# RWKV's outputs: split where they are made instead of stored and loaded again

## The chip, the core and the metric

One core of a Trainium2 chip runs the whole program. The metric is the device time of one execution in microseconds (us). The median of three runs of the kernel before is 2764.43 us (2764.06 to 2771.8).

## What is computed

Two layers over 256 latent and 256 context tokens, width 1024. Each layer has a half-step SwiGLU FFN, three parallel token mixers on one input projection (attention, RG-LRU, RWKV-7), and a second FFN half-step. The change is at the end of the third mixer, where its output is normed per head, gated, and merged with the two others:

```python
def _rwkv_mixer(zr, zrc, mu, w_up, w0, a_up, a0, g_up, k_k, k_a, r_k, ln_g, ln_b, need_ctx):
    ...
    for d in range(2):                                   # both directions
        o_c_d, s_c = _rwkv_scan(s0, rc, w_c, k_c, vc, kkc, a_c, rev)
        o_l_d, _ = _rwkv_scan(s_c, r, w_l, k_l, v, kk, a_l, rev)
        term = o_l_d + _rwkv_bonus(r, k_l, v, r_k)
        o = term if o is None else o + term
    y = (_head_groupnorm(o, ln_g, ln_b) * gate).astype(zr.dtype)

def _gated_merge(outs, zg, proj, w_o):
    g = jax.nn.sigmoid(zg.reshape(zg.shape[0], zg.shape[1], N_BRANCH, D_MODEL))
    acc = g[..., 0, :] * (outs[0] @ proj[0])
    for b in range(1, N_BRANCH):
        acc = acc + g[..., b, :] * (outs[b] @ proj[b])
    return acc @ w_o
```

Context tokens are needed in the first layer only, so the merge runs over 512 columns there and over 256 in the second.

## The kernel before

Activations lie transposed: channels on the 128 partitions, tokens along the free dimension. A mixer's output has 512 channels, in four quarters `f`. All products are made in three passes of a split number: a value is cast to fp32r (`hi`, on ACT) and the rest kept (`lo`, on DVE). `split` (L231) does this for activations, `wload` (L192) for weights, which it loads on SP's queue into three rotating raw tiles `wr`; `wh` and `wl` have two buffers each. `gemm_steps` (L219) issues the three matmuls for each of the k quarters, all on L223.

`rwkv` (L954) is a set of generators that `Weave` lays out on PE by hand, with products of `queue` filled in between: first `tiles` (the gates of the merge, sent to memory as `gd`), then `branch` for the branches 0 (attention) and 1 (RG-LRU). That order is fixed on PE; the other engines' instructions are put in order by the scheduler. `finish` (L1390) ends the mixer: quarters 0 to 2 when their recurrences are done, quarter 3 after the last recurrence `recur(3)`. For each quarter it norms `oc`, multiplies by the gate (L1404) and stores it to `yd` in memory on SP's queue (L1405).

`branch` (L1448) multiplies one branch's output with its projection and adds it, gated, into `acc`. It takes a pair of tiles `yh`, `yl` of four quarters from a pool with two such pairs, and for each quarter loads `yr` from `yd` on ACT's queue (L1456) and splits it:

```python
yh = mp.tile([P, 4, n], F32R, tag="yh", name=f"yh{l}{b}", bufs=2)
yl = mp.tile([P, 4, n], F32R, tag="yl", name=f"yl{l}{b}", bufs=2)
for f in range(4):
    yr = mp.tile([P, n], F32, tag="yr", name=f"yr{l}{b}{f}", bufs=T // n)
    nc.scalar.dma_start(out=yr, in_=yd[b][:, f, qc:])
    split(yh[:, f], yl[:, f], yr)
```

`T // n` is 1 in the first layer and 2 in the second. Then come 8 column tiles `m` of 12 matmuls `bp`; the gates return as `gr` on ACT's queue, and DVE makes `acc` (L1480, branch 0) or `gr` times product (L1482), which POOL adds (L1483). Branch 2, the third, is queued after `rwkv` has ended. `project` (L1485) then loads the stream `x` back from `xd` on ACT's queue (L1495) into memory on the chip that the mixer's tiles held, splits `acc` into `ah`, `al`, and multiplies with `w_out`.

Of the kernel before, what the change touches and what calls it, by code (L numbers as in the profile page):

```python
# [9 lines left out]
F32R = mybir.dt.float32r  # L10
# [5 lines left out]
P = 128  # L16
D = 1024
KD = D // P
T = 512
# [77 lines left out]
def build(tc, a, out, upto=99, dbg=None):  # L97
    nc = tc.nc
    es = ExitStack()
    g = Ctx()  # L100
    with es:
# [13 lines left out]
        def axt(name):  # L115
            return ax.tile([P, T], F32, tag="ax", name=name)
# [102 lines left out]
        def gemm_steps(ps, w, xh, xl, kt, c0=0, c1=T):  # L219
            hi, lo = w  # L220
            for k in range(kt):
                for j, (wt, xt) in enumerate(((hi, xh), (hi, xl), (lo, xh))):
                    nc.tensor.matmul(ps[:, c0:c1], wt[:, k], xt(k)[:, c0:c1],  # L223
                                     start=(k == 0 and j == 0), stop=(k == kt - 1 and j == 2))
                    yield
# [5 lines left out]
        def split(hi, lo, src, eng=None):  # L231
            nc.scalar.copy(hi, src)
            nc.vector.tensor_tensor(lo, src, hi.bitcast(F32), ALU.subtract)
# [16 lines left out]
        for l in range(L):  # L250
            t = vec.tile([P, 2, 72], F32, tag="mT", name=f"mT{l}")
# [311 lines left out]
        def head_bcast(rsE, slot, c0, name):  # L563
            pb = axt(f"hb{name}{slot}")
            nc.tensor.matmul(pb[:, c0:], selT[:, slot], rsE[:].rearrange("p q c -> p (q c)")[:, c0:], start=True, stop=True)
            return pb
# [161 lines left out]
        def step(pe=0.0, area=0.0, dve=0.0, act=0.0, pool=0.0, lag=1, need=()):  # L728


            return pe, area, (dve, act, pool), lag, need
# [219 lines left out]
            v = seg3(ap)  # L951
            return v if d == 0 else v[:, :, ::-1]

        def rwkv(l, rk, z, zd, yd, weave, beside, before_last):  # L954

            full = l < L - 1
            qc = 0 if full else SEG
# [4 lines left out]
            with ExitStack() as ey:  # L962
# [426 lines left out]
                def finish(fs, pool):  # L1389

                    yield step(dve=6.5, act=0.4)
                    rsO = head_rsqrt(pool, pool, "hvo", Y["oss"], qc // P, 1.0 / 64, 64e-5, ALU.add, f"o{l}{fs[0]}")
                    gup = pool.tile([P, T], F32, tag="gup", name=f"gup{l}{fs[0]}")
                    nc.sync.dma_start(out=gup, in_=a["rwkv_g_up"][l])
                    for f in fs:
                        yield step(0.23, 0.5, dve=0.7, act=0.65)
                        pb = head_bcast(rsO, f, qc, f"o{l}")
                        oc = r_[f]
                        nc.vector.tensor_tensor(oc[:, qc:], oc[:, qc:], pb[:, qc:], ALU.mult)
                        nc.scalar.activation(oc[:, qc:], oc[:, qc:], AF.Identity, bias=col(R_LNB + f), scale=col(R_LNG + f))  # L1400
                        yield step(0.85, 2.0, dve=0.7)
                        pg = axt(f"pg{l}{f}")
                        nc.tensor.matmul(pg[:, qc:], gup[:, f * P:(f + 1) * P], sgd[:, qc:], start=True, stop=True)
                        nc.vector.tensor_tensor(oc[:, qc:], oc[:, qc:], pg[:, qc:], ALU.mult)  # L1404
                        nc.sync.dma_start(out=yd[:, f, qc:], in_=oc[:, qc:])  # L1405

                parts = [(-20.0, beside[0](weave.set)), (-18.0, beside[1](weave.set)), (-12.0, setup()), (0.0, outputs())]
                for f in range(4):
# [36 lines left out]
                    done[key], tile_of[key] = 0.0, ps  # L1445
                w = wn_

        def branch(l, b, mp, acc, yd, gd):  # L1448

            qc = 0 if l < L - 1 else SEG  # L1450
            n = T - qc
            yh = mp.tile([P, 4, n], F32R, tag="yh", name=f"yh{l}{b}", bufs=2)
            yl = mp.tile([P, 4, n], F32R, tag="yl", name=f"yl{l}{b}", bufs=2)
            for f in range(4):
                yr = mp.tile([P, n], F32, tag="yr", name=f"yr{l}{b}{f}", bufs=T // n)
                nc.scalar.dma_start(out=yr, in_=yd[b][:, f, qc:])  # L1456
                split(yh[:, f], yl[:, f], yr)
            step = BP_STEP[l]

            def load(m):  # L1460
                return wload(a["branch_proj"][l, b][:, m * P:(m + step) * P], 4)

            def load_gate(m):
                gt = mp.tile([P, n], F32, tag="gt", name=f"gr{l}{b}{m}", bufs=BP_GT[l])
                nc.scalar.dma_start(out=gt, in_=gd[b][:, m, qc:])
                return gt
            ahead = min(BP_GT[l] - 1, KD)
            nxt, gts = load(0), [load_gate(m) for m in range(ahead)]
            for m in range(KD):
                if m + ahead < KD:  # L1470
                    gts.append(load_gate(m + ahead))
                if m % step == 0:
                    ws = nxt
                    nxt = load(m + step) if m + step < KD else None
                w = [t[:, :, m % step * P:(m % step + 1) * P] for t in ws]
                ps = (alt if b == 2 else mmt)(f"bp{l}{b}{m}")
                yield from gemm_steps(ps, w, lambda k: yh[:, k], lambda k: yl[:, k], 4, 0, n)
                gt = gts[m]
                if b == 0:
                    nc.vector.scalar_tensor_tensor(acc[:, m, qc:], gt, 1.0, ps[:, 0:n], ALU.add, ALU.mult)  # L1480
                else:
                    nc.vector.scalar_tensor_tensor(gt, gt, 1.0, ps[:, 0:n], ALU.add, ALU.mult)  # L1482
                    nc.gpsimd.tensor_tensor(acc[:, m, qc:], acc[:, m, qc:], gt, ALU.add)  # L1483
# [72 lines left out]
        for l in range(L):  # L1556
            qc = 0 if l < L - 1 else SEG
            ffn(l, 0, 0, more, (l, 1))
            yd = [dpool.tile([P, 4, T], F32, tag=f"yd{b}", name=f"yd{l}{b}") for b in range(3)]
            gd = [dpool.tile([P, KD, T], F32, tag=f"gd{b}", name=f"gd{l}{b}") for b in range(3)]  # L1560
            zd = dpool.tile([P, 4, T], F32, tag="zd", name=f"zd{l}")
            xd = dpool.tile([P, KD, T], F32, tag="xd", name=f"xd{l}")
            nc.scalar.dma_start(out=xd[:, :, qc:], in_=x[:, :, qc:])
            xp.__exit__(None, None, None)
            with tc.tile_pool(name=f"rk{l}", bufs=1, reuse_waits="tile") as rk:
                z = [None] * 15
                attention(l, yd[0], lambda ap: rwkv_inputs(l, rk, ap, z, zd))
                held["cm"].__exit__(None, None, None)
                done = {}
                queue = [tiles(l, gd, done)]  # L1570

                def fill(n):

                    k = 0
                    while k < n and queue:
                        if next(queue[0], queue) is queue:
                            queue.pop(0)
                        else:
                            k += 1
                    return k  # L1580
                em = ExitStack()
                acc = []

                def before_last():
                    mp = em.enter_context(tc.tile_pool(name=f"mb{l}", bufs=1, side="right", reuse_waits="tile"))
                    acc.append(mp.tile([P, KD, T], F32, tag="acc", name=f"acc{l}"))
                    queue.extend(branch(l, b, mp, acc[0], yd, gd) for b in range(2))
                    acc.append(mp)
                    return mp
                phase[0] = f"r{l}"  # L1590
                with tc.manual_schedule(engines={mybir.EngineType.PE}):
                    weave = Weave(fill, done, (0.226, 0.512) if qc == 0 else (0.118, 0.256))
                    rwkv(l, rk, z, zd, yd[2], weave, lru(l, yd[1], done), before_last)
                    fill(10 ** 6)
                phase[0] = f"m{l}"
            if dbg is not None and upto == l:
                for b in range(3):
                    nc.sync.dma_start(out=dbg["y"][b][:, :, qc:], in_=yd[b][:, :, qc:])
            xp = tc.tile_pool(name=f"xp{l + 1}", bufs=1, reuse_waits="tile")
            x = xp.__enter__().tile([P, KD, T], F32, name=f"x{l + 1}")  # L1600
            queue.append(branch(l, 2, acc[1], acc[0], yd, gd))
            fill(10 ** 6)
            phase[0] = ""
            project(l, acc[0], lambda: (em.close(), hold(l + 1)), xd)
            if dbg is not None and upto == l:
                break
            more = sum([ada(l, 8)] + [ada(l + 1, i) for i in range(3)], []) if l + 1 < L else []
            ffn(l, 1, qc, more, (l + 1, 0) if l + 1 < L else None)
            more = sum([ada(l + 1, i) for i in range(3, 9)], []) if l + 1 < L else []
# [40 lines left out]
```

## Time and profile before

| | before |
|---|---|
| median of three runs | 2764.43 us |
| profiled execution, its own time | 2771.72 us |
| its span | 2769.9 us |
| busy PE, DVE, ACT, POOL | 95%, 63%, 40%, 7% of the span |
| granted TensorE clock, mean | 0.945 of full speed |
| chain that ended last, by engine | PE 19%, DVE 4%, ACT 2%, DMA 1% of the span |
| memory traffic | 318.56 MB read, 20.19 MB written |

Matmuls are pipelined, so PE's busy time is not PE at its peak; a gap is read from the idle time before a matmul, and the clock from the granted share (1.00 is 2.4 GHz, 0.50 is 1.2 GHz). `ACTq` and `SPq` rows are DMA issues. The three branches lie between about 1010 and 1125 us in the first layer, and 2448 and 2535 in the second.

### The profile page before, as it was taken

What the parts mean: (1) busy time and instruction counts of PE and PEld (TensorE: products, weight loads), DVE (VectorE), ACT (ScalarE), POOL (GpSimd) and SP (SyncE); (2) the same over time, 40 slices, a digit from 0 to 9 for tenths busy, and PEclk for the clock granted to TensorE, in tenths of its full rate; (3) what the DMA queues carried; (4) which work ended last, traced back from release to release, by engine and by line L of the source; (5) the groups of instructions that cost most, each with busy time, mean ns of one, the idle gap of its engine ahead of it and who ended that gap; (6) DMA issues with size and microseconds to landing.
All of it is one profiled execution on the core that took longest, in us unless ns stands there. A gap on an engine that the chain in (4) does not pass through costs nothing. (4 is left out here: it accounts for less than half of the span.)

```text
span 2769.9 us, 47656 instructions
## 1 busy us (share of the span) xinstructions
PE 2621.5 (95%) x19761; PEld 2178.9 (79%) x19761; DVE 1732.8 (63%) x2984; ACT 1107.9 (40%) x1817; POOL 191.3 (7%) x197
## 2 busy tenths in 40 slices
PE   7999999999999999999999999999898799887999
PEld 5788888766677777888888978888776588777899
DVE  4867556658756655756654774555757766646565
ACT  4323234337644542332323432323346555433343
POOL 1000002220000001200000100001230000002000
PEclk8999999999889999999999999999999798868999
DMA  7655433123211126825533464544224222126465
GB/s 251 226 159 173 146 104 113 54 69 104 76 44 51 57 84 198 253 62 160 152 108 107 155 184 153 178 148 120 75 77 120 60 76 64 44 80 187 123 183 160
DMA packets 480091, 341.84 MB, mean 123 GB/s; under 512 B 17307, under 2 KB 448884, under 8 KB 479618
## 3 DMA queue, kind: packets, MB, share of 16 engines
q1 hardware_dynamic: 460690, 314.22, 37.6%
q10 hardware_dynamic: 19120, 24.52, 3.1%
q8 instruction: 155, 2.54, 0.4%
q14 instruction: 62, 0.51, 0.1%
q0 software_dynamic: 64, 0.05, 0.0%
HBM read 318.56 MB, written 20.19 MB: 122 GB/s over the span
## 5 line engine op out<-in xcount | busy, mean ns | idle before, releaser
L207 ACT CAST wh<-wr 128x1024 fp32r<-128x1024 f32 (+2 forms) x434 | 436.6, 1008 | 1011.5 <-PE gu L223 353.0
L216 DVE TENSOR_TENSOR wl<-wr,wh 128x1024 fp32r<-128x1024 f32 (+2 forms) x404 | 474.1, 1175 | 291.2 <-ACT wh L207 287.1
L223 PE MATMUL gu<-h_hi,wh 128*128 128x512 f32 (+1 forms) x1528 | 536.9, 353 | 5.7 <-ACT h_hi L389 2.6
L223 PE MATMUL gu<-h_hi,wl 128*128 128x512 f32 (+1 forms) x1528 | 535.6, 351 | 1.7 <-DVE wl L216 1.7
L223 PE MATMUL gu<-h_lo,wh 128*128 128x512 f32 (+1 forms) x1528 | 535.9, 351 | 0.4 <-DVE h_lo L390 0.3
L223 PE MATMUL win<-h_hi,wl 128*128 128x512 f32 (+1 forms) x896 | 331.8, 371 | 3.0 <-DVE wl L216 3.0
L223 PE MATMUL win<-h_hi,wh 128*128 128x512 f32 (+1 forms) x896 | 332.5, 371 | 2.1 <-ACT wh L207 1.7
L223 PEld LDWEIGHTS gu<-h_hi,wh 128*128 128x128 f32 x1528 | 292.1, 192 | 48.7 <-ACT wh L207 6.0
L223 PE MATMUL win<-h_lo,wh 128*128 128x512 f32 (+1 forms) x896 | 329.4, 368 | 0.0
L223 PEld LDWEIGHTS gu<-h_hi,wl 128*128 128x128 f32 x1528 | 293.1, 192 | 39.9 <-DVE wl L216 3.1
L223 PEld LDWEIGHTS gu<-h_lo,wh 128*128 128x128 f32 x1528 | 292.9, 192 | 36.9 <-DVE h_lo L390 0.9
L281 DVE SCALAR_TENSOR_TENSOR adacc<-adw,sc,adacc 128x1024 f32<-128x1024 f32 x196 | 244.7, 1283 | 5.9 <-ACT adacc L279 2.7
L223 PEld LDWEIGHTS win<-h_hi,wl 128*128 128x128 f32 x896 | 176.8, 197 | 44.7 <-issue 21.2
L223 PEld LDWEIGHTS win<-h_hi,wh 128*128 128x128 f32 x896 | 177.1, 198 | 38.0 <-issue 15.8
L223 PEld LDWEIGHTS win<-h_lo,wh 128*128 128x128 f32 x896 | 176.7, 197 | 36.2 <-issue 16.5
L223 PE MATMUL dn<-gh,wh 128*128 128x512 f32 (+1 forms) x560 | 201.0, 359 | 0.0
L223 PE MATMUL dn<-gl,wh 128*128 128x512 f32 (+1 forms) x560 | 199.5, 356 | 0.1
L223 PE MATMUL dn<-gh,wl 128*128 128x512 f32 (+1 forms) x560 | 199.1, 356 | 0.0
L472 DVE SCALAR_TENSOR_TENSOR x<-dn,cf,x 128x256 f32<-128x256 f32 x120 | 53.6, 479 | 113.1 <-PE dn L223 112.8
L506 DVE TENSOR_TENSOR th<-th,gu 128x512 f32<-128x512 f32 (+1 forms) x88 | 54.3, 618 | 111.0 <-PE gu L223 110.6
L223 PEld LDWEIGHTS dn<-gh,wh 128*128 128x128 f32 x560 | 105.2, 188 | 16.9 <-ACT wh L207 1.3
L223 PEld LDWEIGHTS dn<-gh,wl 128*128 128x128 f32 x560 | 105.0, 188 | 16.5
(557 smaller groups left out, 4154.0 us busy)
## 6 DMA issues: line engine op xcount, KB each, us to landing
wr<-ffn_w_gu SPq DMA_DIRECT2D x176, 512.0 KB
adw<-ada_w SPq DMA_DIRECT2D x144, 512.0 KB
wr<-w_in SPq DMA_DIRECT2D x106, 512.0 KB
wr<-ffn_w_d SPq DMA_DIRECT2D x64, 512.0 KB
wr<-ffn_w_d SPq DMA_DIRECT2D x35, 384.0 KB
wr<-w_out SPq DMA_DIRECT2D x17, 512.0 KB
gd<-gt SPq DMA_DIRECT2D x24, 256.0 KB
wr<-branch_proj SPq DMA_DIRECT2D x24, 256.0 KB
```

The source lines that it names most:

```text
L207: nc.scalar.copy(hi[:, 0:w], raw[:, 0:w])
L216: eng.tensor_tensor(lo[:, 0:m], raw[:, 0:m], hi[:, 0:m].bitcast(F32), ALU.subtract)
L223: nc.tensor.matmul(ps[:, c0:c1], wt[:, k], xt(k)[:, c0:c1], start=(k == 0 and j == 0), stop=(k == kt - 1 and j == 2))
L281: nc.vector.scalar_tensor_tensor(acc, w, f, acc, ALU.mult, ALU.add)
L472: nc.vector.scalar_tensor_tensor(x[:, k, cs], ps[:, cs], coef[:, s, k:k + 1], x[:, k, cs], ALU.mult, ALU.add)
L506: nc.vector.tensor_tensor(th[:, c0:], th[:, c0:], pp[1][:, c0:], ALU.mult)
```

## The change

`finish` no longer stores a quarter: it casts and subtracts it at once into the pair `last_y`, which is taken from the pool when the first quarter is ready. `branch` for the third branch gets this pair and loads nothing. The pool keeps two pairs, and `yr` its buffers.

```diff
-        def rwkv(l, rk, z, zd, yd, weave, beside, before_last):
+        def rwkv(l, rk, z, zd, last_y, weave, beside, before_last):
...
                         nc.vector.tensor_tensor(oc[:, qc:], oc[:, qc:], pg[:, qc:], ALU.mult)
-                        nc.sync.dma_start(out=yd[:, f, qc:], in_=oc[:, qc:])
+                        if not last_y:
+                            last_y.extend(pool.tile([P, 4, T - qc], F32R, tag=t, name=f"{t}{l}2", bufs=2) for t in ("yh", "yl"))
+                        split(*[t[:, f] for t in last_y], oc[:, qc:])
...
-        def branch(l, b, mp, acc, yd, gd):
+        def branch(l, b, mp, acc, yd, gd, y=None):
...
-            yh = mp.tile([P, 4, n], F32R, tag="yh", name=f"yh{l}{b}", bufs=2)
-            yl = mp.tile([P, 4, n], F32R, tag="yl", name=f"yl{l}{b}", bufs=2)
-            for f in range(4):
+            yh, yl = y or [mp.tile([P, 4, n], F32R, tag=t, name=f"{t}{l}{b}", bufs=2) for t in ("yh", "yl")]
+            for f in range(0 if y else 4):
...
-                done = {}
+                done, last_y = {}, []
...
-                    rwkv(l, rk, z, zd, yd[2], weave, lru(l, yd[1], done), before_last)
+                    rwkv(l, rk, z, zd, last_y, weave, lru(l, yd[1], done), before_last)
...
-            queue.append(branch(l, 2, acc[1], acc[0], yd, gd))
+            queue.append(branch(l, 2, acc[1], acc[0], yd, gd, last_y))
```

PE's order is the same in the first layer, and nearly so in the second. What moves is on ACT and DVE. In the first layer, on ACT, from the end of branch 0 into branch 1. Before, `yh_9821` is branch 2's and `yr_9823` its first quarter; branch 1's casts into `yh_9613` stand 18 to 30 rows further up:

```order
L1465 DMA gr_9577<-gd_3757 128x512
L207 CAST wh_9633<-wr_9631 128x512
L1465 DMA gr_9637<-gd_3758 128x512
L207 CAST wh_9643<-wr_9641 128x512
L232 CAST yh_9821<-yr_9823 128x512
L1465 DMA gr_9639<-gd_3758 128x512
L207 CAST wh_9666<-wr_9664 128x512
L1456 DMA yr_9827<-yd_3756 128x512
L1465 DMA gr_9662<-gd_3758 128x512
```

Now `yh_9619` is branch 1's, `yr_9621` its first quarter, and `wh_9649` the weights of its second column tile, whose buffer the last tile of branch 0 gives back:

```order
L207 CAST wh_9649<-wr_9647 128x512
L232 CAST yh_9619<-yr_9621 128x512
L1466 DMA gr_9645<-gd_3758 128x512
L1457 DMA yr_9625<-yd_3755 128x512
L232 CAST yh_9619<-yr_9625 128x512
L1457 DMA yr_9629<-yd_3755 128x512
L232 CAST yh_9619<-yr_9629 128x512
L1457 DMA yr_9633<-yd_3755 128x512
L232 CAST yh_9619<-yr_9633 128x512
L207 CAST wh_9672<-wr_9670 128x512
```

All four casts of branch 1 have moved from beside branch 0 to behind it, each behind the load that it needs, and the first of them waits for PE.

The same place of the second layer, on ACT, after the change; `yh_21969` is the third branch's, `yh_22094` branch 1's. Before, two casts of branch 2 stood where the first two of branch 1 now stand, and branch 1's stood further up:

```order
L232 CAST yh_21969<-zr_2_19717 128x256
L207 CAST wh_22128<-wr_22126 128x1024
L232 CAST yh_22094<-yr_22096 128x256
L232 CAST yh_22094<-yr_22100 128x256
L1466 DMA gr_22124<-gd_16798 128x256
L1457 DMA yr_22104<-yd_16795 128x256
L1457 DMA yr_22108<-yd_16795 128x256
L232 CAST yh_22094<-yr_22104 128x256
L232 CAST yh_22094<-yr_22108 128x256
```

Two loads and four casts of branch 1 now stand between branch 0's last weights and the rest; on DVE the first two subtractions stand ahead of a step of the recurrence, the others behind it.

And on ACT where the third branch's last quarter `zr_3` is finished in the second layer, before:

```order
L1400 ACTIVATE zr_3_20703<-zr_3_20703,vb_2323 128x256
L1456 DMA yr_22352<-yd_16808 128x256
L1495 DMA x_22337<-xd_16813 128x8x256
L232 CAST yh_22338<-yr_22352 128x256
L207 CAST wh_22412<-wr_22410 128x1024
```

and now:

```order
L1400 ACTIVATE zr_3_20691<-zr_3_20691,vb_2323 128x256
L232 CAST yh_21969<-zr_3_20691 128x256
L1496 DMA x_22331<-xd_16801 128x8x256
L1466 DMA gr_22367<-gd_16799 128x256
L1466 DMA gr_22384<-gd_16799 128x256
```

The load is gone and the cast stands directly behind the quarter's last values.

## Rows read from the trace of the kernel before

**Rows 1.** Stretches: length, busy PE PEld DVE ACT POOL (count), clock, DMA, GB/s.
```profile
...
1072.00:1100.00 28.00, 24.49 (x93) 18.64 (x92) 13.99 (x19) 6.35 (x12) 10.02 (x7) 0.88 0.71 218
...
2500.00:2520.00 20.00, 10.67 (x74) 9.54 (x73) 11.87 (x28) 3.56 (x6) 3.16 (x4) 0.84 0.54 161
...
```

**Rows 2.** Who waited for whom, PE, 1000 to 1130: us, times, longest.
```profile
...
PE bp L223 <- DVE acc L1480: 3.4, 1, 3.4
...
```

**Rows 3.** The same, PE, 2440 to 2600.
```profile
...
PE bp L223 <- ACT yh L232: 11.1, 3, 6.1
...
```

**Rows 4.** The same, SP's queue, 1000 to 1130.
```profile
...
SPq L201 <- DVE wl L216: 61.2, 22, 7.5
...
```

**Rows 5.** Timeline, first layer, branch 0's loads and casts: start, length, engine [idle <-releaser].
```profile
...
1018.18 0.33 ACTq L1456 DMA_DIRECT2D yr<-yd  x1
...
1021.20 0.62 ACT L232 CAST yh<-yr 128x512 fp32r<-128x512 f32 x1 [0.30 <-DMA yr<-yd]
...
1031.62 0.33 ACTq L1456 DMA_DIRECT2D yr<-yd  x1
...
```

**Rows 6.** Timeline, first layer, from branch 0 to branch 1.
```profile
...
1064.29 0.34 SPq L1405 DMA_DIRECT2D yd<-zr  x1
...
1067.44 0.40 ACTq L1495 DMA_DIRECT2D x<-xd  x1
...
1072.02 0.61 ACT L232 CAST yh<-yr 128x512 fp32r<-128x512 f32 x1
...
1076.91 0.69 DVE L1480 SCALAR_TENSOR_TENSOR acc<-gr,bp 128x512 f32<-128x512 f32 x1 [6.66 <-DMA gr<-gd]
...
1077.74 0.76 PE L223 MATMUL bp<-yh,wh 128*128 128x512 f32 x1 [3.39 <-DVE acc L1480]
...
1078.12 0.68 DVE L233 TENSOR_TENSOR yl<-yr,yh 128x512 fp32r<-128x512 f32 x1
...
```

**Rows 7.** Timeline, second layer, from branch 0 to branch 1.
```profile
...
2489.97 0.79 ACT L232 CAST yh<-yr 128x256 fp32r<-128x256 f32 x2
...
2490.16 1.22 DVE L216 TENSOR_TENSOR wl<-wr,wh 128x1024 fp32r<-128x1024 f32 x1
...
2491.38 0.42 DVE L1482 SCALAR_TENSOR_TENSOR gr<-gr,bp 128x256 f32<-128x256 f32 x1
...
2493.10 0.37 ACTq L1456 DMA_DIRECT2D yr<-yd  x1
...
2495.73 0.41 DVE L1353 SCALAR_TENSOR_TENSOR zr<-pmn,zr 128x256 f32<-128x256 f32 x1
...
2497.01 0.41 ACT L232 CAST yh<-yr 128x256 fp32r<-128x256 f32 x1 [2.46 <-DMA yr<-yd]
...
2497.32 0.41 ACT L1356 ACTIVATE z<-zr 128x256 f32<-128x256 f32 x1
...
2497.45 0.43 DVE L233 TENSOR_TENSOR yl<-yr,yh 128x256 fp32r<-128x256 f32 x1 [0.97 <-ACT yh L232]
...
```

**Rows 8.** Timeline, second layer, the third branch's last quarter.
```profile
...
2512.91 0.42 DVE L1404 TENSOR_TENSOR zr<-zr,pg 128x256 f32<-128x256 f32 x1 [0.67 <-ACT zr L1400]
...
2515.26 0.33 ACTq L1456 DMA_DIRECT2D yr<-yd  x1
...
2517.82 0.41 ACT L232 CAST yh<-yr 128x256 fp32r<-128x256 f32 x1 [4.94 <-DMA yr<-yd]
...
2518.28 0.79 PE L223 MATMUL bp<-yh,wh 128*128 128x256 f32 x2 [6.06 <-ACT yh L232]
...
```

**Rows 9.** Stretches behind PE's two gaps, columns as in rows 1.
```profile
...
1077.74:1083.00 5.26, 5.26 (x13) 4.09 (x14) 2.26 (x4) 0.81 (x2) 1.66 (x1) 0.50 0.77 223
1083.00:1100.00 17.00, 16.88 (x71) 12.90 (x70) 10.90 (x14) 4.91 (x9) 8.36 (x6) 0.99 0.62 176
2518.28:2527.12 8.84, 8.31 (x36) 8.02 (x37) 5.08 (x8) 3.31 (x6) 4.50 (x5) 0.50 0.72 215
2527.12:2530.00 2.88, 2.88 (x25) 2.88 (x25) 2.58 (x7) 1.76 (x3) 0.86 (x1) 0.97 0.65 193
...
```

More of the change, by code (lines that the diff above doesn't have):

```diff
@@ L1596, in build @@
             if dbg is not None and upto == l:
-                for b in range(3):
+                for b in range(2):
                     nc.sync.dma_start(out=dbg["y"][b][:, :, qc:], in_=yd[b][:, :, qc:])
```

## The prediction

> **What bounds the kernel now.** I read the page first: PE is busy over 95% of the span, so a change outside PE's path is worth only what it does to PE's gaps. Next the stretches around the three branches of both layers. In the first layer PE is idle for 3.5 us of the 28 between 1072 and 1100; in the second it is busy for only 10.67 us of the 20 between 2500 and 2520 [rows 1]. Then what PE waited for there: in the first layer one wait of 3.4 us, for DVE's `acc` [rows 2], which itself waited for a gate tile; in the second 11.1 us for ACT's `yh`, the longest 6.1 [rows 3]. These 6.1 us are what the change aims at. The third branch's last quarter is finished on DVE at 2513.33 (2512.91 and 0.42), goes out, is asked back at 2515.26, is cast at 2517.82, and PE starts at 2518.28: 4.95 us from the last value to its first product [rows 8]. In the first layer PE's list of waits has none for `yh`, so there is no such gap to win. Last I read what a branch's loads and splits cost when nothing hides them [rows 5 to 7], since the order shows that their place moves.
>
> **What the change moves.** *The way through memory.* Eight stores on SP and eight loads on ACT go, four of each in a layer; the eight casts and eight subtractions stay, at the values' birth. On SP the stores were not what held the weights: in the stretch of the first layer the weight loads waited 22 times, 61.2 us in all, for DVE to give back a raw tile [rows 4]. I cost the issues at nothing. The later splits of branch 0 in the first layer now come between the third branch's own, closer to their products; the gate products that PE still has to do hide them, and I cost that at nothing too. If that cover is gone, PE waits for a cast and a subtraction, 0.62 and 0.68 [rows 5, 6], 1.3 us.
>
> *The pairs of tiles.* There are two `yh`/`yl` pairs. Before, branches 0 and 1 had one each, and branch 2 took over branch 0's while branch 1 was multiplied. Now the third branch holds one pair from its first quarter on, branch 0 has the other, and **branch 1 has to wait for branch 0's last matmul** before it can split anything. The order says so: its first cast stands behind the weight cast that waits for that matmul, in the place where branch 2's first cast stood. What PE does next needs it at once. In place of one late wait the change sets two.
>
> **First layer, between branches 0 and 1.** The raw tile `yr` has one buffer here, so a load can start only when the split before it is done. The period from load to load is 4.48 us: three of them reach from 1018.18 to 1031.62, with 3.02 us from issue to cast [rows 5]. Before, all of that ran beside other products. Now only the first of four loads is early.
> - The first cast can start at 1072.02, as branch 2's did [rows 6]. Its subtraction stands on DVE behind the last `acc`, which waits until 1076.91 for a gate tile queued behind the 2 MB of `x`, and behind one `wl`: that subtraction ended at 1078.80 [rows 6]. `x` waited for the store issued at 1064.29 until 1067.44 [rows 6]; now it waits for a split, and I take 0.7 us off: 1078.1.
> - Three more quarters in series: 3 x 4.48 = 13.4, so the fourth is split at 1091.5.
> - Its three matmuls run at the lower clock, as after the 3.39 us gap (13 in 5.26 us, granted 0.50) [rows 9]: 1.3 us. The second tile of branch 1 then starts at 1092.8, where it started at 1077.74 [rows 6]: **+15.1 us**.
> - The lower clock afterwards was there before too, for 5.26 us; in the second layer it lasted 8.84 [rows 9]. Half of the 3.6 us between them is the most that can be added: 0 to 1.8, and I take 0.5, since the gaps are longer than the old one. **+15.6**.
>
> The bounds. Low: the gate tile comes in time, so the first subtraction ends at 1073.3, and a load takes 2.56 us, as the half-sized one did [rows 8]: 1073.3 + 3 x 4.0 + 0.7 is 1086.0, so +8. High: the subtraction ends at 1078.8, and the clock's whole 1.8: +17.6. I take the value near the upper end, because the order leaves that gate wait and the `x` load where they were. By the Trainium skill, "DMA: Bandwidth & Descriptors", "Anatomy of one DMA", a transfer costs about 2.0 us and its bytes at 436 GB/s, 2.6 us for 256 KB by a fit made on another issue path; the trace's own load took 3.02, and by the page's figure the sum would be 1.3 us less.
>
> **Second layer, between branches 0 and 1.** `yr` has two buffers, so two quarters are ready. Two casts of `yh` ran at 2489.97; the `wl` that DVE does first took 2490.16 to 2491.38 [rows 7]. The first subtraction, 0.43 [rows 7], ends at 2491.8 and frees the load of the third quarter. That load took 3.9 us in this stretch (2493.10 to 2497.01) [rows 7], 2.56 at the end [rows 8]; with 3.4 the third is cast at 2495.3 and the fourth ends its products by 2496.9. Before, they ended as `gr` began, at 2491.38 [rows 7]: +5.5 (4.1 to 6.0). PE's order has the last step of the recurrence behind them, and the third branch's last quarter comes from it, so this delay goes into that chain. The next 24 matmuls at the lower clock (0.245 instead of 0.115 us each) [rows 9] would add 3.1, or nothing if the clock holds; I take 2.2. The chain then gets 1.2 us back, as L1356 no longer stands behind a cast that waited for its load until 2497.01 [rows 7]. So the last quarter is finished 6.5 us later, at 2519.8.
>
> Then the change pays: no store, no load, and PE starts a cast (0.41) later, at 2520.3 instead of 2518.28, **+2.0**. With PE's gap cut to about 2 us the clock should hold: before, 36 matmuls took 8.84 us at 0.50, and at 0.115 they would take 4.1 [rows 9]; 4.7 can come back. DVE and POOL still have `gr`, `wl` and `al` to do, so I take half, 2.3. Net **-0.3**, from -6.2 (4.1 - 1.2 - 4.4 - 4.7) to +4.7 (6.0 + 3.1 - 4.4, no slack, no clock).
>
> **Sum.** 15.6 - 0.3 = +15.3 us. Behind both places PE is the full engine, so nothing takes it back. On the profiled execution, 2771.72, that is 2787.0. That execution lies 7.3 above the median of the three runs, which is what I go by: 2764.43 + 15.3 = **2779.7**. A difference under about 0.3%, 8.3 us, can't be told from none here.
>
> **Rivals.**
> - *The waits are cheap (0.12):* the first layer at its low end, +8, the second at its low end, -6: **+2, 2766.4**. For it: both low ends are durations that occur. Against: it needs the gate tile 3 us sooner. A change that merely shuffles waits and leaves the time, as it would if branch 1 found a free pair after all and the first layer kept its other waits, ends here too.
> - *Faster (0.06):* branch 1's loads and splits end before branch 0's last tile, that is before 1072.0 [rows 6] and 2490.0 [rows 7]. Then only the gains remain: `x` starts 3.15 us sooner and the gate wait of 3.39 goes with its 2.2 us of lower clock; in the second layer 4.4 for the round trip and 4.7 for the clock. Together -14.7, **2749.7**. It decides if a third pair is there when branch 1 is written; the two buffers and the order speak against it. The same page of the Trainium skill, same section, puts most of a DMA's fixed 2 us down to the receipt of its last bytes, a cost of every transfer whatever its size, and by that 16 transfers fewer are a gain. In these rows only the last of them is waited for.
> - *The clock stays down (0.06):* the first layer's four broken pieces keep TensorE at the lower of its levels (1.2 against 2.4 GHz) for branch 1's seven other tiles: 84 matmuls at 0.405 instead of 0.239 us [rows 9], +14 more: **2794**. Against: after the 3.39 us gap it recovered within 5.26 us.
>
> **The numbers.** The forecast gets 0.71: with its bounds, +9 to +22. What is left, 0.05, is slower by a cause that I don't see. The cheap waits are no change, the fast rival is faster, the rest slower: faster 0.06, same 0.12, slower 0.82. For 8 in 10 I leave out the fast rival and the low clock, and reach down over half of the cheap waits: 2769 to 2788.
>
> **What would show it.** Right: between branches 0 and 1 of the first layer three loads of `yr` some 4.4 us apart, with three matmuls after each and PE waiting about 14 us for `yh` and `yl`; in the second layer a wait of some 4 us for `yh` before 2497, and the 6 us wait for the last quarter down to about 2, with the clock near 1.0 behind it. Wrong: branch 1's casts done before branch 0's last matmul; a period well under 4 us; PE's wait for the last quarter gone while the chain before it did not move.

## The result, and the profile after

The changed kernel takes 2781.72 us, median of 5 runs (2778.19 to 2788.73), against 2764.43 for the kernel before in the same comparison: ratio 1.0057, 95% interval 1.0037 to 1.0076, 10 to 21 us slower. Forecast were 2779.7 us, in a range of 2769 to 2788. The profiled execution of the changed kernel, 2778.19 us (span 2776.4), is the fastest of its five, and that of before, 2771.72, the slower end of its own. Their difference, 6.5 us, is therefore not the cost of the change; I compare stage by stage.

The first view is PE's list of waits, in the first layer (1000 to 1145) and then in the second (2440 to 2610): who waited for whom, us in all, times, longest.

```profile
PE bp L223 <- ACT yh L232: 9.3, 4, 3.5
PE bp L223 <- DVE yl L233: 3.3, 1, 3.3
...
PE bp L223 <- ACT yh L232: 11.4, 5, 3.5
```

In the first layer the one wait of 3.4 us for `acc` [rows 2] has become four for `yh` and one for `yl`, 12.6 us. In the second, the sum for `yh` is what it was, 11.1 [rows 3] and 11.4, but no wait is longer than 3.5. The longest, 3.5, and one of 1.8 are branch 0's own and were there before (3.5 and 1.5; `yring` below comes back to them). What has changed is the rest: 1.4 and 3.2 for branch 1 are new, and the 6.1 us for the last quarter have become 1.6.

The timeline of the first layer, from branch 0's last products (PE ends them at 1068.35) to the second tile of branch 1; columns are start, length, engine, line, operation, out<-in and, in brackets, the idle time before it with its releaser.

```profile
1060.66 0.69 DVE L233 TENSOR_TENSOR yl<-zr,yh 128x512 fp32r<-128x512 f32 x1 [0.69 <-ACT yh L232]
...
1061.38 0.33 ACTq L1496 DMA_DIRECT2D x<-xd  x1
...
1069.34 0.50 PE L223 MATMUL bp<-yh,wh 128*128 128x512 f32 x1 [0.99 <-ACT yh L232]
...
1071.24 0.69 DVE L1481 SCALAR_TENSOR_TENSOR acc<-gr,bp 128x512 f32<-128x512 f32 x1 [4.95 <-DMA gr<-gd]
...
1072.45 0.68 DVE L233 TENSOR_TENSOR yl<-yr,yh 128x512 fp32r<-128x512 f32 x1
...
1073.16 0.33 ACTq L1457 DMA_DIRECT2D yr<-yd  x1
...
1076.88 0.62 ACT L232 CAST yh<-yr 128x512 fp32r<-128x512 f32 x1 [7.60 <-DMA yr<-yd]
...
1078.26 0.33 ACTq L1457 DMA_DIRECT2D yr<-yd  x1
...
1081.27 0.62 ACT L232 CAST yh<-yr 128x512 fp32r<-128x512 f32 x1 [3.77 <-DMA yr<-yd]
...
1082.65 0.33 ACTq L1457 DMA_DIRECT2D yr<-yd  x1
...
1085.57 0.62 ACT L232 CAST yh<-yr 128x512 fp32r<-128x512 f32 x1 [3.68 <-DMA yr<-yd]
...
1086.22 0.69 DVE L233 TENSOR_TENSOR yl<-yr,yh 128x512 fp32r<-128x512 f32 x1 [3.61 <-ACT yh L232]
...
1087.99 0.63 PE L223 MATMUL bp<-yh,wh 128*128 128x512 f32 x1
```

Three times the same sequence: load, cast, subtraction, next load. No load is issued before the subtraction ahead of it has given back the one raw buffer. Branch 1's second tile starts 19.6 us behind branch 0's last product, where it was 6.3 before, from 1071.47 to 1077.74 [rows 6]. The first of these two is the start of branch 1's first product in the kernel before, directly behind branch 0's last, in PE's timeline:

```profile
1071.47 0.39 PE L223 MATMUL bp<-yh,wh 128*128 128x512 f32 x1
```

The stretches around both places: length, busy PE PEld DVE ACT POOL (count), granted clock, DMA share, GB/s.

```profile
1068.35:1088.00 19.65, 7.04 (x13) 3.19 (x14) 3.96 (x6) 2.99 (x6) 0.00 (x0) 0.63 0.41 122
1088.00:1090.55 2.55, 2.55 (x8) 1.97 (x6) 1.29 (x2) 0.42 (x1) 1.55 (x1) 0.50 0.00 0
1090.55:1110.00 19.45, 19.45 (x87) 16.11 (x86) 12.01 (x14) 4.34 (x7) 9.17 (x8) 1.00 0.61 174
...
2503.14:2507.03 3.89, 3.89 (x20) 3.38 (x21) 1.59 (x4) 0.29 (x1) 0.72 (x1) 0.50 0.02 4
...
2527.11:2531.82 4.71, 2.48 (x13) 2.19 (x13) 2.11 (x6) 1.04 (x1) 2.77 (x4) 0.56 0.54 162
2531.82:2537.72 5.90, 5.86 (x25) 5.57 (x26) 4.72 (x7) 2.86 (x7) 0.78 (x1) 0.50 0.98 293
```

The clock comes back 2.55 us behind the long gap of the first layer (5.26 us before [rows 9]), and the tiles that follow run without any gap, 19.45 busy of 19.45. In the second layer it is low for 3.9 us behind branch 1's waits, and low again for 10.6 us from the third branch's start, a gap of 2.23 us included (8.84 us before [rows 9]).

There, the timeline of the second layer:

```profile
2495.68 0.42 DVE L1481 SCALAR_TENSOR_TENSOR acc<-gr,bp 128x256 f32<-128x256 f32 x1 [1.12 <-PE bp L223]
...
2498.29 0.81 ACTq L1457 DMA_DIRECT2D yr<-yd  x2
...
2502.68 0.75 ACT L232 CAST yh<-yr 128x256 fp32r<-128x256 f32 x2 [5.40 <-DMA yr<-yd]
...
2505.07 0.42 DVE L1483 SCALAR_TENSOR_TENSOR gr<-gr,bp 128x256 f32<-128x256 f32 x1 [1.18 <-PE bp L223]
...
2526.20 0.42 DVE L1404 TENSOR_TENSOR zr<-zr,pg 128x256 f32<-128x256 f32 x1 [0.67 <-ACT zr L1400]
...
2527.11 0.77 PE L223 MATMUL bp<-yh,wh 128*128 128x256 f32 x4 [1.61 <-ACT yh L232]
...
2531.82 0.58 PE L223 MATMUL bp<-yh,wh 128*128 128x256 f32 x1 [2.23 <-ACT wh L207]
```

Branch 1's first `gr` comes 9.4 us behind branch 0's last `acc`. The third branch's first product now stands 0.91 us behind the start of the last value's multiplication, not 5.37 [rows 8].

For all kernels below I use four lengths of the profiled executions, named L0 and L1 by the layer (L1404 and the like are lines). First layer (L0): from the start of RWKV's last product with `pg` (L1404) to the first residual addition `x<-wo00b` (L472); it holds the end of branch 0 and the two others. Second layer (L1), each from the start of RWKV's last `pq` matmul (L1193; its last start stands in the line's own view): to the last L1404, to the first `x<-wo`, to the end of the span. For the changed kernel the rows are

```profile
1059.29 0.68 DVE L1404 TENSOR_TENSOR zr<-zr,pg 128x512 f32<-128x512 f32 x1
...
1138.47 0.48 DVE L472 SCALAR_TENSOR_TENSOR x<-wo00b,cm,x 128x256 f32<-128x256 f32 x1 [0.60 <-PE wo00b L223]
...
2544.54 0.48 DVE L472 SCALAR_TENSOR_TENSOR x<-wo,cm,x 128x256 f32<-128x256 f32 x1 [0.62 <-PE wo L223]
```

and `pq` last starts at 2439.0 (before: 2432.8). "Measured" is the ratio to before, times that comparison's median of before, which was 2764.43 for the changed kernel and 2754.96, 2755.38 and 2755.07 in the three sets of experiments.

| kernel | ratio [95% interval] | measured us | L0 | L1 to L1404 | to `x<-wo` | to the end |
|---|---|---|---|---|---|---|
| before | 1 | 0 | 66.5 | 80.1 | 102.9 | 337.1 |
| changed | 1.0057 [1.0037, 1.0076] | +15.8 (the medians differ by 17.3) | 79.2 | 87.2 | 105.5 | 337.4 |
| `l1only` | 1.0006 [0.9985, 1.0027] | +1.7 | 67.0 | 86.5 | 104.4 | 335.9 |
| `l0only` | 1.0043 [1.0025, 1.0062] | +11.8 | 78.9 | 80.1 | 102.7 | 335.1 |
| `swap0` | 1.0009 [0.9991, 1.0027] | +2.5 | 66.8 | 86.6 | 104.4 | 335.7 |
| `three_l1` | 1.0020 [0.9998, 1.0042] | +5.5 | 78.6 | 78.6 | 96.5 | 328.2 |
| `before3` | 1.0002 [0.9975, 1.0029] | +0.6 | 67.5 | 79.1 | 102.2 | 337.2 |
| `l1only3` | 0.9961 [0.9938, 0.9984] | -10.7 | 66.4 | 78.8 | 96.7 | 327.8 |
| `swap0_three_l1` | 0.9961 [0.9938, 0.9983] | -10.7 | 66.8 | 78.6 | 96.4 | 328.1 |
| `yring` | 0.9956 [0.9936, 0.9975] | -12.1 | 69.8 | 75.9 | 91.8 | 324.4 |
| `yring_l1` | 0.9992 [0.9965, 1.0018] | -2.2 | 79.2 | 74.7 | 90.4 | 324.1 |
| `before_ring` | 1.0021 [0.9995, 1.0047] | +5.8 | 73.1 | 73.6 | 96.5 | 330.9 |
| `yring_three_l1` | 0.9943 [0.9920, 0.9966] | -15.7 | 72.2 | 72.0 | 88.9 | 321.1 |
| `swap0_ring_three_l1` | 0.9942 [0.9915, 0.9968] | -16.0 | 66.2 | 72.2 | 89.0 | 321.4 |

L0 and the last column together, less those of before, give the measured difference within 6 us in every row, and inside its interval: to that precision the change and all its variants act in these two stages. A length itself is good to 1 to 2.4 us: equal first layers in different kernels give 66.4 to 67.5, 78.6 to 79.2, and 69.8 and 72.2 with the ring; the changed second layer gives 337.4, 335.9 and 335.7, the one before 337.1 and 335.1.

### The profile page after: what moved, and what is told of

Same layout as the page of the kernel before. It is cut to its first block, busy times and chain, and to the rows that moved or that the text cites. A ratio compares the mean times of both kernels' runs of the same rounds, so it can differ in the third digit from the quotient of the medians.

```text
span 2776.4 us, 47619 instructions
## 1 busy us (share of the span) xinstructions
PE 2620.6 (94%) x19761; PEld 2177.6 (78%) x19761; DVE 1733.9 (62%) x2984; ACT 1109.0 (40%) x1817; POOL 191.0 (7%) x197
## 5 line engine op out<-in xcount | busy, mean ns | idle before, releaser
L472 DVE SCALAR_TENSOR_TENSOR x<-dn,cf,x 128x256 f32<-128x256 f32 x120 | 53.6, 480 | 112.1 <-PE dn L223 111.9
```

The costliest lines, as they stand in the source:

```text
L472: nc.vector.scalar_tensor_tensor(x[:, k, cs], ps[:, cs], coef[:, s, k:k + 1], x[:, k, cs], ALU.mult, ALU.add)
```

## The experiments

The theory under test: the cost lies in the first layer, where branch 1 must wait for branch 0's pair and then brings in its quarters one after the other; in the second layer the same wait is paid back by the third branch's early start.

**One layer at a time** (`l1only`; `l0only` has the condition the other way round).

```diff
+                        if not (not full):
+                            nc.sync.dma_start(out=yd2[:, f, qc:], in_=oc[:, qc:])
+                            continue
                         if not last_y:
```

> The change in the second layer alone; the first layer's third branch goes through memory as before. Theory (the cost is the first layer's serial way: with one pair of split tiles taken early, branch 1's four quarters are loaded, cast and subtracted one after the other behind branch 0's last matmul): about the time before, 2764 to 2768 us, with the 6.3 us from branch 0's last tile to branch 1's first tile back in layer 0. Rival A (the pair taken early costs as much in the second layer, where the last quarter comes 6.5 us later): about 2771 us, 6 to 7 above before. Rival B (the cost is in neither boundary but in the casts and subtractions put into the last outputs of RWKV, on ScalarE and VectorE): half of the cost of the whole change, 2772 to 2774.

> The change in the first layer alone; the second layer's third branch goes through memory as before. Theory: nearly the whole cost of the change, 12 to 15 us above before, 2776 to 2780 us, with the three serial loads at the boundary of branch 0 and branch 1. Rival A (second layer): 2771 or less. Rival B (outputs' splits): 2772 to 2774. Together with the run of the second layer alone: if the two costs add up to the whole change's 17 us, nothing is lost between the layers; if they come short of it, some of it is not in the two stages.

Measured: +1.7 and +11.8 us. The whole cost is the first layer's; the second layer's is nothing that can be told from zero (interval -4 to +7). Rival A expected 2771 us for the second layer alone, 6 to 7 above before, and is at the edge of that interval; its premise, the later chain, is in the trace (86.5 for 80.1), but the first `x<-wo` comes only 1.5 us later. Rival B, equal halves, lies just outside it (the upper end is 2771.9), and `swap0` below excludes it. The two add up to 13.5 us, inside the interval of the whole.

**The branches in the order 0, 2, 1 in layer 0** (`swap0`).

```diff
+                queue.append(branch(l, 2, acc[1], acc[0], yd, gd, last_y, taken(l, 1, acc[1], yd, y1)))
+                queue.append(branch(l, 1, acc[1], acc[0], yd, gd, y1))
...
                     nc.gpsimd.tensor_tensor(acc[:, m, qc:], acc[:, m, qc:], gt, ALU.add)
+                next(beside, None)
```

`taken` loads and splits one quarter of branch 1 at each step, four in all.

> The whole change, and in layer 0 the branches in the order 0, 2, 1: the third branch, whose split is already on the chip, directly behind branch 0, and branch 1's loads and splits into branch 0's pair beside the third branch's matmuls. No buffer more, no instruction more. Theory (it is the wait for the pair and the serial loads, not the splits themselves): the 19.8 us from the last tile of branch 0 to the next tile shrink to the 2 us of a tile that nothing holds up, no stretch at the half clock behind it: 17.8 us and 1 to 2 us of slow matmuls less than the changed kernel, 2761 to 2764 us. Rival B (the splits in the outputs hold TensorE up): as the changed kernel, 2779 to 2782. Rival C (the serial quarters are only moved: they take 4.4 us each also beside the matmuls, and delay the third branch's gate loads on ScalarE's queue): 2766 to 2774.

Measured: +2.5 us over before, 13 us less than the changed kernel, in L0 12.4 less. The waits for `yh` and `yl` are gone from the first layer's list, which shows their cause; the splits in the outputs are still there, so rival B is out. But 18 to 20 us were expected, so a third of the expected gain is missing. The time, about 2767 us with an interval of 2762 to 2772, lies in rival C's range; by the time alone the theory's 2764 is not excluded either. PE's list of waits in that layer now begins with

```profile
PE bp L223 <- DVE wl L216: 2.7, 4, 0.9
```

and two stretches behind branch 0's end show 2.4 us of PE idle in each:

```profile
1068.00:1093.00 25.00, 22.60 (x90) 16.20 (x90) 12.65 (x20) 5.91 (x10) 10.49 (x8) 1.00 0.60 183
1093.00:1120.00 27.00, 24.63 (x111) 18.59 (x109) 16.10 (x23) 9.04 (x15) 12.20 (x9) 1.00 0.68 203
```

In the changed kernel PE had no gap behind its wait. My reading is that there weights and gates had run ahead while PE stood still, so that part of a long wait is paid back by what it lets run ahead; no run isolates this. Rival C's picture is in the trace too, with branch 1's casts 4.7 to 8.2 us apart beside the third branch's matmuls, but PE's one listed wait for a gate product is 0.6 us. Which of the two takes the missing third stays open.

**A third pair in the second layer** (`three_l1`; the first layer has no room for one).

```diff
-... name=f"{t}{l}{b}", bufs=2) for t in ("yh", "yl")]
+... name=f"{t}{l}{b}", bufs=2 if l == 0 else 3) for t in ("yh", "yl")]
```

> The whole change, with three pairs of split tiles instead of two in the second layer (there is room for a third pair there, not in the first layer). Theory (in the second layer the chain comes 6.5 us later since branch 1's first tile waits for branch 0's pair): the last quarter is ready at about the time before, the third branch starts without its wait of 6 us, 7 to 10 us less than the changed kernel: 2772 to 2775 us. Rival A (the later chain comes from the order on ScalarE, not from the pair): 0 to 2 us less, 2780 to 2782.

Measured: +5.5 over before, 10.3 less than the changed kernel. The last L1404 comes 8.6 us earlier, 1.5 before its old place, and the end of the span 9.2. That is a little more than the theory's 7 to 10. The pair was what held the chain; rival A is out.

**The common ring** (`yring`).

```diff
-yr = mp.tile([P, n], F32, tag="yr", ..., bufs=T // n)
+yr = mp.tile([P, n], F32, tag="gt", ..., bufs=BP_GT[l] + T // n)
...
-gt = mp.tile([P, n], F32, tag="gt", ..., bufs=BP_GT[l])
+gt = mp.tile([P, n], F32, tag="gt", ..., bufs=BP_GT[l] + T // n)
```

> The whole change, with the loads of the quarters and of the gates in one ring of buffers (three in layer 0, six in layer 1; the same memory, since the quarters' own buffers go), so that a quarter's load no longer waits for the subtraction of the quarter before it. The pair still waits for branch 0's last matmul. Theory: in layer 0 the first cast stands behind branch 0 as it did, the other three follow as their loads arrive instead of 4.4 us apart: the second tile of branch 1 comes 8 to 12 us earlier, and the kernel lies 6 to 10 us under the changed one, 0.1 to 0.4% above before. Rival (the 4.4 us are not the one buffer's but the queue's, busy with the gates and the weights): the quarters stay 4 us apart and the time stays 0.5 to 0.6% above before.

Measured: 12.1 us less than before, 28 less than the changed kernel. L0 is 9.4 shorter, as expected (7.0 in `yring_three_l1`, whose first layer is the same): that is the single raw buffer's share of the 12.7 us, and what is left is the wait for the pair. But L1 is 13 shorter, which nobody expected. The timeline of PE and ScalarE in the second layer of the kernel before shows where half of it comes from:

```profile
2447.76 0.58 ACT L1227 COPY bt<-pz 32x512 f32<-32x512 f32 x1 [1.13 <-PE pz L1224]
2447.77 0.84 ACTq L1456 DMA_DIRECT2D yr<-yd  x2
...
2451.20 0.58 PE L223 MATMUL bp<-yh,wh 128*128 128x256 f32 x1 [3.48 <-ACT yh L232]
...
2452.25 0.85 ACTq L1456 DMA_DIRECT2D yr<-yd  x2
...
2455.24 0.58 PE L223 MATMUL bp<-yh,wh 128*128 128x256 f32 x1 [1.53 <-ACT yh L232]
...
2457.27 3.68 PE L1276 MATMUL pu<-W,bt 64*64 64x128 f32 x32
...
2466.68 1.17 ACT L1279 COPY W<-pu 64x512 f32<-64x512 f32 x2 [1.67 <-PE pu L1276]
```

and of `yring`:

```profile
2442.55 0.58 ACT L1227 COPY bt<-pz 32x512 f32<-32x512 f32 x1 [1.13 <-PE pz L1224]
2442.56 1.99 ACTq L1457 DMA_DIRECT2D yr<-yd  x4
...
2445.83 0.58 PE L223 MATMUL bp<-yh,wh 128*128 128x256 f32 x1 [3.31 <-ACT yh L232]
...
2449.93 2.12 PE L1276 MATMUL pu<-W,bt 64*64 64x128 f32 x32
...
2455.23 1.17 ACT L1279 COPY W<-pu 64x512 f32<-64x512 f32 x2 [0.48 <-PE pu L1276]
```

In PE's fixed order branch 0's first 13 products stand between RWKV's products `pz`, which give `bt`, and `pu`, and the copies `W` wait for `pu`. Before, branch 0's loads go out two at a time and PE waits twice for its casts; with the ring all four go out at once, and the second wait is gone. From the last `bt` to `pu` it is 9.5 us before, 7.4 with the ring. The larger part is the clock. From `pu` to the last `W`, before and with the ring (columns as above):

```profile
2457.27:2466.68 9.41, 9.41 (x72) 7.97 (x71) 1.17 (x3) 4.29 (x9) 0.00 (x0) 0.50 0.16 47
...
2449.93:2455.23 5.30, 5.30 (x72) 4.52 (x72) 1.29 (x4) 3.47 (x6) 0.00 (x0) 0.97 0.22 69
```

The same 72 matmuls take 9.4 us at the lower level and 5.3 near the upper. It is so in every trace: the median `pu` takes 0.417 us in the nine kernels without the ring in this layer and 0.269 in the five with it. So of the 6.2 us from the last `bt` to the last `W` (18.9 to 12.7), 2.1 are the wait and 4.1 the clock behind it. A wait of a branch that nobody needs yet stood in front of the chain that everybody waits for. It stood on PE: the expectation of `yring_l1` below puts it on ScalarE, where the casts come ahead of `W`, but what ScalarE waits for before `W` is `pu`.

**A third pair without the way on the chip** (`before3`, the kernel before with the same `bufs`).

> The kernel before, with three pairs of split tiles in the second layer. Theory (a third pair is worth something only where a branch waits for a pair and not for its data; before, the third branch waits for its last quarter's way through memory): within 3 us of before. Rival (a third pair helps by itself, through branch 1's earlier splits): 5 to 9 us less than before.

Measured: +0.6, L1 as before. The interval, -7 to +8, leaves the rival little room. PE's list has the same three waits for `yh` in the second layer (2423 to 2600):

```profile
PE bp L223 <- ACT yh L232: 10.8, 3, 5.9
```

Before it was 11.1, 3, 6.1 [rows 3]. The two shorter ones are branch 0's, the longest is the third branch's for its data; a third pair shortens none of them.

**The second layer alone, with three pairs** (`l1only3`).

> The change in the second layer alone, and three pairs there; the first layer as before. Theory (in the second layer the way on the chip is worth the 6 us wait of the third branch, once the pair it takes early doesn't hold branch 1 up): 6 to 9 us less than before, ratio 0.9968 to 0.9978. Rival (the three pairs' gain in the run with them was the gain of branch 1 alone, as a third pair gives it to the kernel before too): the same time as the kernel before with three pairs.

Measured: 10.7 less than before (interval -17 to -4, 6 to 9 expected), L1 9.3 shorter; the rival is out. Way and pair together give what neither gives alone (+1.7 and +0.6).

**Order 0, 2, 1 and three pairs** (`swap0_three_l1`).

> Both repairs together: branches 0, 2, 1 in layer 0, three pairs in layer 1, all on the chip. If the two add up as measured apart against the changed kernel (13 and 10 us): 5 to 7 us less than before, ratio 0.9975 to 0.998. Rival (they overlap through the clock or through the weights' prefetch between the layers): within 3 us of before.

Measured: 10.7 less than before, L0 as before and L1 9.0 shorter, so the two add up: 13 and 10 off +15.8 are -7, inside the interval (-17 to -5). The rival's 3 us lie outside it.

**The ring in the second layer alone** (`yring_l1`).

> The whole change with the common ring in the second layer alone; layer 0 as the changed kernel has it. The common ring gave 28 us against the changed kernel where 6 to 10 were expected, and its trace shows 9.4 us of it in layer 0 and about 13 in layer 1, where RWKV's copies W<-pu on ScalarE come 6.5 us sooner behind the last bt copy: they had stood on ScalarE behind branch 0's casts, which waited for their loads two at a time. Theory: 10 to 16 us under the changed kernel, ratio to before 1.000 to 1.002. Rival (the gain came from the first layer, or from the two together): 1.004 or more.

Measured: 2.2 under before, 18 under the changed kernel, 2 more than the theory's upper end; L0 is that of the changed kernel, 79.2, and L1 is 13.3 shorter. The interval's upper end, 1.0018, excludes the rival.

**The ring in the kernel before** (`before_ring`).

> The kernel before, third branch through memory, with the common ring in both layers. Theory (branch 0's casts held RWKV's copies up before the change as well, 18.9 us from the last bt copy to the last W copy, as after it): 6 to 9 us less than before, 0.9967 to 0.9978. The distance to the changed kernel with the same ring (0.9956) is then what the way on the chip is worth where the loads don't wait: 3 to 6 us. Rival 1 (the ring only makes good what the change had spoilt): the time before. Rival 2 (the ring does all, and the way on the chip nothing): 0.9956.

Measured: +5.8, with an interval of -1 to +13. The expectation missed. In the second layer it holds: L1404 6.5 us earlier, the end 6.2. But L0 is 6.6 longer, which I had not looked for. In the ring a branch's quarters stand behind the gates of the branch ahead, and their first load goes out only when that branch is nearly done. So PE waits at the start of branch 1 (1059.99 and 1064.06) and again at that of the third branch (1087.97):

```profile
1052.91 0.33 ACTq L1456 DMA_DIRECT2D yr<-yd  x1
...
1059.99 0.50 PE L223 MATMUL bp<-yh,wh 128*128 128x512 f32 x1 [2.40 <-ACT wh L207]
...
1064.06 0.79 PE L223 MATMUL bp<-yh,wh 128*128 128x512 f32 x1 [2.62 <-ACT yh L232]
...
1084.00 0.33 ACTq L1456 DMA_DIRECT2D yr<-yd  x1
...
1087.97 0.49 PE L223 MATMUL bp<-yh,wh 128*128 128x512 f32 x1 [0.71 <-ACT yh L232]
```

In all of L0 PE is idle for 10.7 us of 73.1, before for 6.2 of 66.5. Rival 1 has the time right and the reason wrong: the ring gains in one layer what it loses in the other. With the third branch on the chip only the two other branches' quarters are in the ring, and `yring` loses less there (69.8). In L1 the way on the chip is worth 6.5 us with the ring (330.9 to 324.4).

**Ring and three pairs; and with the order 0, 2, 1** (`yring_three_l1`, `swap0_ring_three_l1`).

> The whole change, the common ring in both layers and three pairs in the second. Theory: the wait for the pair, 5.7 us from branch 0's last tile to branch 1's first in layer 1 with the ring alone, goes to about 2, and the kernel comes to 0.9935 to 0.9948 of before. Rival (with the ring the chain of RWKV sets the third branch's start in layer 1, and branch 1 only waits elsewhere): 0.9950 to 0.9960, as the ring alone.

> All three: common ring, three pairs in the second layer, branches 0, 2, 1 in layer 0. In layer 0 the stretch from RWKV's last product to the last tile of the last branch is 63.4 us with the order 0, 2, 1 and 66.4 with the ring: theory, 3 to 5 us less than the ring with three pairs, the best of all kernels here, 0.992 to 0.994. Rival (in the order 0, 2, 1 the tiles are held by the gates' and weights' loads, one tile ahead, and branch 1's quarters now come into the same ring as the gates): no gain over the ring with three pairs, or a loss of up to 3 us.

Measured: 15.7 and 16.0 less than before. The first is as its theory said, L1 3.3 shorter again. The second has the shortest L0, 66.2 for 72.2, but no shorter time: by the times, the rival. An interval of 14 us can't tell 4 us, so it stays open what the order gives on top. These two are the fastest kernels here, and both are faster than before; the simpler of them is the ring with three pairs.

## Why the prediction was right

The mechanism, the place and the sign were right. By its steps:

- *The pair.* Branch 1's first cast waits for branch 0's last matmul in both layers: shown by the rows, by `swap0` and by `three_l1`.
- *The first subtraction.* Forecast 6.6 us behind branch 0's last product (1078.1 against 1071.47), it ended 4.8 behind it (1073.13 against 1068.35). The term was mis-sized: I let the `x` load go out 0.7 us earlier, and against branch 0's end it went out 2.9 earlier (7.0 ahead of it, at 1061.38; before 4.0, at 1067.44 [rows 6]), directly behind a subtraction and no longer behind a store. The gate tile queued behind it came earlier too.
- *Three serial quarters, 13.4 us.* From the first subtraction's end to the fourth's: 13.8. Three slow matmuls, 1.3: measured 1.1. The loads took 3.7, 3.0 and 2.9 us from issue to cast. By the Trainium skill, "DMA: Bandwidth & Descriptors", "Anatomy of one DMA", 256 KB would take 2.6 us, an estimate by a fit made on another issue path; the rows lie 0.3 to 1.1 above it, and the forecast's 3.02 [rows 5] was the better price.
- *Sum at the boundary.* Forecast +15.1, measured 19.6 - 6.3 = +13.3.
- *The clock behind it.* Forecast +0.5. It was low for 2.55 us, not 5.26, so this was a gain. The whole first layer: forecast +15.6, measured +12.7 in the trace and +11.8 in the times of `l0only`.
- *Second layer, the last quarter 6.5 us later:* 7.1. Its parts were further off: branch 1's first tile +7.2 instead of +5.5 (9.4 from `acc` to `gr`, 2.2 before), as the third quarter's load took 4.4 us to its cast (2498.29 to 2502.68), not 3.4, and the low clock began inside that tile. The 20 matmuls of the low stretch cost 1.6 instead of 2.2 (3.89 us, 2.3 at 0.115 each); as part of them lies in the first tile, the two overlap.
- *The round trip, -4.4:* from the start of L1404 to PE, 5.37 became 0.91, -4.5.
- *The clock behind it, -2.3:* failed. I had expected it near 1.0; it was 0.56, then 0.50 until 2537.7, and a second gap of 2.23 us for the weights' cast came in between. So the +2.6 us that 7.1 and -4.5 leave are still there at the first `x<-wo`: the term was 0.
- *Second layer in sum, -0.3:* +0.3 to the end of the span. The missing 2.3 us came back later, where the forecast said that nothing takes anything back. 1.7 of them lie inside the output product, between its first and its last `x<-wo`: 24.2 us for 25.9, PE's longest wait for `wh` there 2.0 us for 2.8, and the granted clock 0.93 for 0.87. It is not chance of one trace: that stretch takes 23.7 and 23.5 in `l1only` and `swap0`, both at 1.00, and 25.5 in `l0only`, at 0.87. What shortens the stretch no experiment asks; so this sum is right partly by compensation.
- *The total, +15.3:* measured +15.8, between 10 and 21. That it fits so closely is partly luck: the two stages add up to 13.0 in the trace, and `l0only` and `l1only` to 13.5.
- *Issues and SP's queue at nothing:* the runs show no cost of them. What I did not see is that branch 0's wait for its casts, which the change leaves alone, held RWKV's chain up on PE, at the lower clock: the ring takes 6.2 us out of the second layer without the change and 13 with it, of which 3.7 are branch 1's first tile (5.7 us behind branch 0's for 9.4); the last 3 I have not traced.

Of the rivals, the fast one named its condition rightly: with a third pair the second layer gives 9.3 us (337.1 to 327.8), for 4.4 and 4.7 forecast; but 3.1 of them come only behind the first `x<-wo` (6.2 up to there). Its first layer, 5.6 us, was not to be had: with the wait gone, L0 is 66.2 to 66.8 us, as before, and the tiles then wait for weights (2.7 us in `swap0`'s list). In the first layer the low clock did not stay, and the cheap waits would have needed the first subtraction 3 us sooner and shorter loads.

## What to carry to other kernels

Whoever makes a value live earlier takes a buffer earlier: ask who had that buffer next, what that one now waits for, and whether a second single buffer (here `yr`) turns the wait into a series. A direct way on the chip and the buffer it occupies belong to one change; in the second layer the way alone was worth nothing that can be told from zero, the third pair alone neither, and both 11 us. And look in the fixed order of the busiest engine for work that waits for a load ahead of work on the critical chain, and for the clock behind that wait: letting those loads go out together, with no more memory, took 6.2 us out of the second layer without the change and 13 with it, where the change aimed at 6.1. A shared ring has its price too: in the first layer of the kernel before it cost 6.6 us, since a branch's loads then stood behind the gates of the branch ahead.

## What was not expected of the hardware

- After 19.65 us in which PE ran 13 matmuls, at a granted 0.63 in the mean, the lower of its two levels (1.2 and 2.4 GHz) lasted another 2.55 us; after a single gap of 3.39 it lasted 5.26 [rows 9]. The longer standstill did not mean the longer return.
- A short second gap kept a whole chain at the lower level: with a wait of 1.53 us among branch 0's 13 products the 72 matmuls behind them ran at 0.50, without it at 0.97 (`yring`).
- Executions differ by more than the change is worth, also ahead of the stages that it touches. RWKV's last product of the first layer started at 1063.57 before, at 1059.29 in the changed kernel and at 1039.36 in `swap0_ring_three_l1`, and the five runs of the changed kernel spread over 10.5 us. 35 runs of the kernel before spread over 39 us, from 2732.85 at a mean granted clock of 0.960 to 2771.87 at 0.945. Spans of two traces therefore can't be subtracted here; stages can, to the 1 to 2.4 us said above.
